# Branch B of the first half, first group: its transposes back and what follows them are released 16 units of the emission clock later

## The chip, the cores and the metric

The kernel runs on one core of one Trainium2 chip. The time is the device time of one execution, in microseconds (us). The program is fixed when it is built: each engine (TensorE, here PE; VectorE, DVE; ScalarE, ACT; GpSimd, POOL; and SyncE's queue SP, which issues the transfers) works through its own list of instructions in order, and engines wait for each other by semaphores.

## The reference, cut to what matters

One layer over 2048 positions with a model width of 1024. An input projection feeds three mixers, their outputs are gated, concatenated, projected back and normalised with the residual. The change touches branch B, whose width is 256:

```
def _conv_module(val, glu_gate, w_dw, b_dw, ln_g, ln_b):
    h = val * jax.nn.sigmoid(glu_gate)
    h = lax.conv_general_dilated(h, w_dw[:, None, :], window_strides=(1,), padding=[(CONV_WIDTH - 1, 0)], ...) + b_dw
    h = _layernorm(h, ln_g, ln_b)
    return jax.nn.silu(h)
...
y_b = _conv_module(b_val, b_glu, conv_w, conv_b, conv_ln_g, conv_ln_b) * jax.nn.silu(b_g)
```

The convolution runs over positions, for each channel by itself, with 31 taps; the layer norm runs over the 256 channels of a position.

## The kernel before, in words

The 2048 positions are worked in two halves (`hf`) of two groups (`gi`) of 512 positions each. In a half, `branch_b` projects for branch B, `sgu` does branch A (both halves, but in the second it comes last), `values` projects the values of branch C (tiles `pm_ci`, eight of them: four for group 0, four for group 1), and `hgrn_unit` does branch C head by head (tiles `pm_f`, `pm_q`, `pm_cg`). Every projection of a 512-wide tile is 8 steps of three matmuls, since each float32 operand is split into a high and a low part (`whi`, `wlo`, `xhi`, `xlo`; on lines 147 and 148 ACT casts the high part of a newly loaded weight and DVE subtracts to get the low one).

The convolution is done by DVE with channels on the partitions: 31 instructions for each pair of group and channel block `ct`, most of them those of line 285 on the tile `acc`. The layer norm needs channels along the free dimension, so `branch_b_norm` has four parts for a group. `part(0)` and `part(1)`, for two of the four 128-position blocks each, transpose `acc` on PE into a PSUM bank `bt`, take mean and variance on DVE (`bst`, `bmv`), the power -0.5 on POOL (`brs`), and write the normalised `bhn` on DVE (line 324). `back(0)` and `back(1)`, for one channel block each, transpose `bhn` back on PE into the bank `bb` (line 330, four transposes of 128x128, which read all four blocks, so the results of both parts), apply SiLU with scale and bias on ACT (`bsy`, line 333), multiply by the gate on DVE (line 334) and store to DRAM through SP (line 232).

Where these parts stand among the other work of an engine is set while the program is written out, by a clock of the builder that has no tie to the time on the chip:

```
def later(dt, fn):
    heapq.heappush(queue, (clock[0] + dt, order[0], fn))
...
def tick(dt):
    clock[0] += dt
    while queue and queue[0][0] <= clock[0]:
        heapq.heappop(queue)[2]()
```

Each step of three 512-wide matmuls is followed by `tick(0.64)`, and whatever has come due is written out at that point. When the last tap of a group has been written out, `conv_taps` puts the four parts into the queue, due after 8, 16, 24 and 32 units (`DNORM` is 8), and a note that the group is done, at 32. The transposes are pinned: PE executes them at the place in its list where they were written out.

Of the kernel before, what the change touches and what calls it, by code (L numbers as in the profile page):

```python
# [42 lines left out]
WB = 5  # L43
NWARM = 9
FIRST = ("00", "x0", "x1", "10", "x2", "01", "x3", "x4", "11", "x5", "x6", "x7")
DTAP, DNORM, DWO = (1.5, 1.35), 8.0, 2.5
DST0, DST, DKT, DPST, DPO, DPT = 4.5, 5.5, 2.5, 2.0, 2.5, 6.0


# [35 lines left out]
def _body(tc, nc, d, ctx):  # L85
# [16 lines left out]
    def bank(tag, bufs, name, shape=(P, 512)):  # L102
        t = ps.tile([P, 512], F32, tag=tag, bufs=bufs, name=name)
        return t
# [15 lines left out]
    def vcol(o):  # L120
        return vec[:, o : o + 1]
# [60 lines left out]
    def later(dt, fn):  # L182
        heapq.heappush(queue, (clock[0] + dt, order[0], fn))
        order[0] += 1
# [11 lines left out]
    def pinned(m):  # L196
        tc.keep_in_program_order(m)
        return m
# [26 lines left out]
    def rstd_of(pl, mv_var, n, tag, scale=1.0, bufs=3):  # L225
        r = pl.tile([P, n], F32, tag=tag, bufs=bufs, name=tag)
        nc.gpsimd.tensor_scalar(r, mv_var, scale, EPS, ALU.mult, ALU.add)  # L227
        nc.gpsimd.tensor_tensor(r, r, nhalf[:, :n], ALU.pow)  # L228
        return r

    def y_store(et, g, t):
        nc.sync.dma_start(y_dr[et, :, g * G : (g + 1) * G], t)
# [37 lines left out]
    def conv_taps(hf, pl, hs, sbg):  # L270
        def normed():
            conv_done[hf] = conv_done.get(hf, 0) + 2

        for gi in range(GPH):
            acc = {}
            for ct in range(2):
                while (ct, gi) not in hs:
                    yield False
                h = hs[ct, gi]
                a = pl.tile([P, G], F32, tag="acc", bufs=4, name=f"acc{hf}_{gi}_{ct}")  # L280
                cw = V_CW + ct * CW
                nc.vector.tensor_scalar(a, h[:, 0:G], vcol(cw), vcol(V_CB + ct), ALU.mult, ALU.add)
                yield True
                for k in range(1, CW):
                    nc.vector.scalar_tensor_tensor(a, h[:, k : k + G], vcol(cw + k), a,  # L285
                                                   ALU.mult, ALU.add)
                    yield True
                acc[ct, gi] = a
            parts = branch_b_norm(hf, pl, sbg, acc, gi)
            for k, part in enumerate(parts):  # L290
                later(DNORM * (k + 1), part)
            later(DNORM * len(parts), normed)

    def conv_start(hf, pl, hs, sbg):
        it = conv_taps(hf, pl, hs, sbg)
        due = [clock[0]]

        def step():
            r = next(it, None)
            if r is not None:  # L300
                due[0] = due[0] + DTAP[hf] if r else clock[0] + DTAP[hf]
                later(due[0] - clock[0], step)

        later(0, step)

    def branch_b_norm(hf, pl, sbg, acc, gi):
        g = hf * GPH + gi
        hn = pl.tile([P, 4, 256], F32, tag="bhn", bufs=1, name=f"bhn{g}")

        def part(cp):  # L310
            mv = pl.tile([P, 2, 2], F32, tag="bmv", bufs=2, name=f"bmv{g}_{cp}")
            pt = bank(("o", "st")[cp], 1, f"bt{g}_{cp}").rearrange("p (c f) -> p c f", f=256)
            for cc in range(2):
                c = cp * 2 + cc
                for ct in range(2):
                    pinned(nc.tensor.transpose(pt[:, cc, ct * P : (ct + 1) * P],
                                               acc[ct, gi][:, c * P : (c + 1) * P], ident))
            for cc in range(2):
                bst = pl.tile([P, 6], F32, tag="bst", bufs=4, name=f"bst{g}_{cp}_{cc}")
                nc.vector.bn_stats(bst, pt[:, cc, :])  # L320
                nc.vector.bn_aggr(mv[:, cc, :], bst)
            rs = rstd_of(pl, mv[:, :, 1], 2, "brs")
            for cc in range(2):
                nc.vector.tensor_scalar(hn[:, cp * 2 + cc, :], pt[:, cc, :], mv[:, cc, 0:1],
                                        rs[:, cc : cc + 1], ALU.subtract, ALU.mult)

        def back(ct):
            pb = bank("tr", 1, f"bb{g}_{ct}")
            for c in range(4):
                pinned(nc.tensor.transpose(pb[:, c * P : (c + 1) * P],  # L330
                                           hn[:, c, ct * P : (ct + 1) * P], ident))
            sy = pl.tile([P, G], F32, tag="bsig", bufs=2, name=f"bsy{g}_{ct}")
            nc.scalar.activation(sy, pb, AF.Silu, bias=vcol(V_CLB + ct), scale=vcol(V_CLG + ct))
            nc.vector.tensor_mul(sy, sy, sbg[ct, gi])
            y_store(2 + ct, g, sy)

        return [lambda: part(0), lambda: part(1), lambda: back(0), lambda: back(1)]
# [713 lines left out]
```

## Time and profile before

| | |
|---|---|
| runs, us | 927.38, 927.51, 928.24 (median 927.51) |
| profiled execution, us | 927.59 |
| its span, first to last instruction, us | 925.8 |
| PE busy | 904.1 us, 98% |
| DVE busy | 713.8 us, 77% |
| ACT busy | 392.2 us, 42% |
| POOL busy | 81.2 us, 9% |
| mean granted clock of TensorE | 0.994 of full speed |

The profiled execution takes 1.79 us more than its span: that much lies before the first and behind the last instruction. Matmuls are pipelined, and their ends are modelled: the duration of a matmul in the rows is longer than the distance to the next one, so work on PE is best counted from start to start. A time in brackets at the end of a row is how long the engine stood idle before it, and whom it waited for. A group of transposes that PE works through in one go is one row with its count.

### The profile page before, as it was taken

The page shows a single profiled execution, that of the slowest core. Times are in us where ns is not written, and L with a number is a line of the kernel's source. Part 1 is how long each engine was busy: PE and PEld are TensorE (multiplying, and loading weights), DVE is VectorE, ACT ScalarE, POOL GpSimd, SP SyncE. Part 2 cuts the span into 40 slices and gives each one's busy share as a digit, 9 for nine tenths or more (in the row PEclk, how much of TensorE's full clock was granted, in tenths as well). Part 3 has the DMA queues.
Part 4 walks back from the last instruction along what each step waited for, and adds up shares of the span by engine and source line. Part 5 has one row for each costly group of instructions (what it writes and reads, how often), then busy time and mean ns, then how long its engine had stood idle before and what let it go on. Part 6 is the DMA issues. An engine that isn't in the chain of part 4 may idle for free.

```text
span 925.8 us, 15037 instructions
## 1 busy us (share of the span) xinstructions
PE 904.1 (98%) x5673; PEld 738.2 (80%) x5673; DVE 713.8 (77%) x1614; ACT 392.2 (42%) x774; POOL 81.2 (9%) x127
## 2 busy tenths in 40 slices
PE   9999998899999999999999999999999999999996
PEld 6889886787777887888888887887889888888885
DVE  5998899935688768997999777778786135898777
ACT  6624355143435336644314334444553343543450
POOL 0001200100010000001000000001012000221122
PEclk9999999899999999999999999999999999999999
DMA  7506786120102103421202011111151498455322
GB/s 259 185 25 224 257 297 248 55 91 24 46 35 69 47 13 110 147 91 64 66 3 92 24 68 36 57 36 58 36 182 58 156 347 292 160 182 183 135 92 91
DMA packets 60808, 107.43 MB, mean 116 GB/s; under 512 B 5312, under 2 KB 21952, under 8 KB 60608
## 3 DMA queue, kind: packets, MB, share of 16 engines
q1 hardware_dynamic: 60736, 106.48, 33.7%
q8 instruction: 44, 0.72, 0.3%
q14 instruction: 28, 0.23, 0.1%
HBM read 75.00 MB, written 31.46 MB: 115 GB/s over the span
## 4 chain that ended last, share of the span: by engine, by line
PE 74%; DVE 13%; DMA 4%; issue 3%; ACT 3%; POOL 2%; SPq 0%; POOLq 0%; DVEq 0%; ACTq 0%
DVE acc L285 5%; PE pm_q L201 3%; PE poz L201 3%; PE poz L203 3%; PE poz L202 3%; PE pm_q L203 3%; PE pm_q L202 3%; PE pm_f L201 3%; PE pm_ci L201 3%; PE pm_ci L203 3%; PE pm_ci L202 3%; PE pm_cg L201 3%; PE pm_f L203 3%; PE pm_f L202 3%; PE pm_cg L202 2%
## 5 line engine op out<-in xcount | busy, mean ns | idle before, releaser
L285 DVE SCALAR_TENSOR_TENSOR acc<-bh,vec,acc 128x512 f32<-128x512 f32 x240 | 172.3, 753 | 2.6
L148 DVE TENSOR_TENSOR wl<-rw,wh 128x512 fp32r<-128x512 f32 x84 | 57.0, 690 | 27.3 <-ACT wh L147 27.1
L147 ACT CAST wh<-rw 128x512 fp32r<-128x512 f32 x84 | 49.9, 618 | 40.7 <-PE pm_f L202 11.1
L201 PE MATMUL pm_f<-xhix,wh 128*128 128x512 f32 x96 | 41.1, 429 | 0.0
L201 PE MATMUL pm_q<-xhix,wh 128*128 128x512 f32 x96 | 40.6, 423 | 0.0
L560 ACT ACTIVATE jk<-po 128x128 f32<-128x128 f32 x64 | 17.7, 277 | 51.9 <-PE po L555 50.9
L201 PE MATMUL pm_cg<-xhix,wh 128*128 128x512 f32 x96 | 39.0, 406 | 0.0
L203 PE MATMUL pm_f<-xhix,wl 128*128 128x512 f32 x96 | 37.7, 393 | 0.0
L202 PE MATMUL pm_q<-xlox,wh 128*128 128x512 f32 x96 | 37.7, 392 | 0.0
L203 PE MATMUL pm_q<-xhix,wl 128*128 128x512 f32 x96 | 37.7, 392 | 0.0
L202 PE MATMUL pm_f<-xlox,wh 128*128 128x512 f32 x96 | 37.6, 392 | 0.0
L203 PE MATMUL pm_cg<-xhix,wl 128*128 128x512 f32 x96 | 37.5, 391 | 0.0
L202 PE MATMUL pm_cg<-xlox,wh 128*128 128x512 f32 x96 | 37.5, 391 | 0.0
L201 PE MATMUL pm_ci<-wh_ci,xhix 128*128 128x512 f32 x96 | 37.4, 389 | 0.0
L203 PE MATMUL pm_ci<-wh_ci,xlox 128*128 128x512 f32 x96 | 37.4, 389 | 0.0
L202 PE MATMUL pm_ci<-wl_ci,xhix 128*128 128x512 f32 x96 | 37.4, 389 | 0.0
L227 POOL TENSOR_SCALAR crs<-ss 128x4 f32<-128x4 f32 x16 | 3.3, 205 | 367.6 <-ACT jk L560 367.6
L355 ACT COPY vh<-pm_ci 128x512 f32<-128x512 f32 x16 | 9.4, 588 | 58.9 <-PE pm_ci L203 58.9
L446 DVE COPY_PREDICATED ST<-msk,sc 64x192 f32<-64x192 int32 (+2 forms) x96 | 28.8, 300 | 5.4 <-PE sc L440 3.1
L503 ACT COPY ST<-sc 64x128 f32<-64x128 f32 x32 | 8.3, 260 | 50.9 <-PE sc L500 50.7
L565 ACT ACTIVATE os<-po,crs 128x128 f32<-128x128 f32 x64 | 18.3, 368 | 24.6 <-POOL crs L228 24.6
L201 PE MATMUL pm_av<-wh_av,xhix 128*128 128x256 f32 x96 | 28.2, 293 | 0.0
(355 smaller groups left out, 2753.1 us busy)
## 6 DMA issues: line engine op xcount, KB each, us to landing
rw<-wf SPq DMA_DIRECT2D x84, 256.0 KB, 3.2
wob<-wo_dr SPq DMA_DIRECT2D x14, 1024.0 KB, 11.5
xr<-x SPq DMA_DIRECT2D x16, 512.0 KB, 3.8
ry<-y_dr SPq DMA_DIRECT2D x32, 256.0 KB, 2.8
out<-xr SPq DMA_DIRECT2D x15, 512.0 KB, 2.6
wo_dr<-wsh SPq DMA_DIRECT2D x28, 256.0 KB, 3.2
wo_dr<-wsl SPq DMA_DIRECT2D x28, 256.0 KB, 2.9
rx<-xT SPq DMA_DIRECT2D x24, 256.0 KB, 3.4
```

The lines of the kernel that those rows point to most:

```text
L147: nc.scalar.copy(hi, src)
L148: nc.vector.tensor_sub(lo, src, hi.bitcast(F32))
L201: nc.tensor.matmul(out, wh, xh, start=first, stop=False, **kw)
L202: nc.tensor.matmul(out, wh, xl, start=False, stop=False, **kw)
L203: nc.tensor.matmul(out, wl, xh, start=False, stop=last, **kw)
L227: nc.gpsimd.tensor_scalar(r, mv_var, scale, EPS, ALU.mult, ALU.add)
L285: nc.vector.scalar_tensor_tensor(a, h[:, k : k + G], vcol(cw + k), a, ALU.mult, ALU.add)
L355: nc.scalar.copy(vh[:, gi * 4 + tt, :], pt)
L446: nc.vector.copy_predicated(ST[rr, :, 64 * m + j0 * b : 64 * m + (j0 + nj) * b], msk[rr, mo : mo + mw].unsqueeze(1).to_broadcast([64, 4, mw]),
L503: nc.scalar.copy(ST[0:64, e:4:2, 64:128], pcv[64 * e : 64 * e + 64])
L560: nc.scalar.activation(jk, po[:, c * P : (c + 1) * P], AF.Square, accum_out=ss[:, c : c + 1])
L565: nc.scalar.mul(os_[:, c * P : (c + 1) * P], po[:, c * P : (c + 1) * P], rs[:, c : c + 1])
```

## The change

The two parts that transpose back, and the note that the group is done, are put into the queue with 16 units more, in the first half's first group alone. The two parts ahead of them keep their due times (8 and 16), and the other three groups keep all of theirs.

```
-DTAP, DNORM, DWO = (1.5, 1.35), 8.0, 2.5
+DTAP, DNORM, DBACK, DWO = (1.5, 1.35), 8.0, 16.0, 2.5
...
             parts = branch_b_norm(hf, pl, sbg, acc, gi)
+            gap = DBACK if hf == 0 and gi == 0 else 0.0
             for k, part in enumerate(parts):
-                later(DNORM * (k + 1), part)
-            later(DNORM * len(parts), normed)
+                later(DNORM * (k + 1) + (gap if k > 1 else 0.0), part)
+            later(DNORM * len(parts) + gap, normed)
```

The due times of this group become 8, 16, 40 and 48. Sixteen units are 25 steps of 0.64, so 75 matmuls. One line more in the file moves later line numbers by one. The lists of POOL and SP hold the same instructions in the same order as before; PE, ACT and DVE differ only in where the two `back` parts stand.

**PE, before, at the first transposes back.** The names say: `pm_ci_0_1` is the second tile of the values (group 0), `pm_ci_0_2` the third; the last number of a name only tells buffers apart.

```order
L201 MATMUL pm_ci_0_1_1572<-wh_ci_3_1504,xhi_first 128x512
L202 MATMUL pm_ci_0_1_1572<-wl_ci_3_1505,xhi_first 128x512
L203 MATMUL pm_ci_0_1_1572<-wh_ci_3_1504,xlo_first 128x512
L330 MATMUL bb_0_1615<-ident,bhn_1308 128x128 x4
L201 MATMUL pm_ci_0_2_1625<-wh_ci_0_1474,xhi_first 128x512
L202 MATMUL pm_ci_0_2_1625<-wl_ci_0_1475,xhi_first 128x512
L203 MATMUL pm_ci_0_2_1625<-wh_ci_0_1474,xlo_first 128x512
```

**PE, now, at the first transposes back.** `pm_ci_1_1` is the sixth tile of the values (group 1).

```order
L201 MATMUL pm_ci_1_1_1732<-wh_ci_0_1474,xhix_266 128x512
L202 MATMUL pm_ci_1_1_1732<-wl_ci_0_1475,xhix_266 128x512
L203 MATMUL pm_ci_1_1_1732<-wh_ci_0_1474,xlox_267 128x512
L331 MATMUL bb_0_1736<-ident,bhn_1308 128x128 x4
L201 MATMUL pm_ci_1_1_1732<-wh_ci_0_1474,xhix_266 128x512
L202 MATMUL pm_ci_1_1_1732<-wl_ci_0_1475,xhix_266 128x512
L203 MATMUL pm_ci_1_1_1732<-wh_ci_0_1474,xlox_267 128x512
```

So `bb_0` stands behind 24 + 24 + 24 + 3 = 75 more matmuls of the values (all of `pm_ci_0_2`, `pm_ci_0_3` and `pm_ci_1_0`, one step of `pm_ci_1_1`). `bb_1` moves by as many, from behind the fifth step of `pm_ci_0_3` to behind the sixth step of `pm_ci_1_2`. With each group of four transposes move its SiLU on ACT, its product on DVE and its store.

**DVE, before, from the last taps of the second group to the weights of branch C.** `acc_1_1` is the second channel block of the half's second group, `bsy` the result of a `back` part, `wl_0` low parts of weights for branch C.

```order
L285 SCALAR_TENSOR_TENSOR acc_1_1_1790<-bh_1_577,vec,acc_1_1_1790 128x512 x4
L334 TENSOR_TENSOR bsy_0_1620<-bsy_0_1620,sbg_0_264 128x512
L285 SCALAR_TENSOR_TENSOR acc_1_1_1790<-bh_1_577,vec,acc_1_1_1790 128x512 x11
L334 TENSOR_TENSOR bsy_1_1697<-bsy_1_1697,sbg_0_516 128x512
L285 SCALAR_TENSOR_TENSOR acc_1_1_1790<-bh_1_577,vec,acc_1_1_1790 128x512 x9
L148 TENSOR_TENSOR wl_0_1860<-rw_0_0_1861,wh_0_1859 128x512
L148 TENSOR_TENSOR wl_0_1860<-rw_0_1_1865,wh_0_1859 128x512
```

**DVE, now, the same stretch.**

```order
L285 SCALAR_TENSOR_TENSOR acc_1_1_1781<-bh_1_577,vec,acc_1_1_1781 128x512 x24
L335 TENSOR_TENSOR bsy_0_1741<-bsy_0_1741,sbg_0_264 128x512
L335 TENSOR_TENSOR bsy_1_1798<-bsy_1_1798,sbg_0_516 128x512
L148 TENSOR_TENSOR wl_0_1860<-rw_0_0_1861,wh_0_1859 128x512
L148 TENSOR_TENSOR wl_0_1860<-rw_0_1_1865,wh_0_1859 128x512
```

The two products move behind all 24 remaining taps, and stand directly ahead of the low parts of the weights for branch C.

## Rows read from the trace of the kernel before

**Rows 1.** The page: span; busy time, share and instructions of each engine.

```profile
span 925.8 us, 15037 instructions
...
PE 904.1 (98%) x5673; PEld 738.2 (80%) x5673; DVE 713.8 (77%) x1614; ACT 392.2 (42%) x774; POOL 81.2 (9%) x127
```

**Rows 2.** Waits of PE, whole span: total us, times, longest us.

```profile
PE bb L330 <- DVE bhn L324: 3.5, 1, 3.5
PE pk L515 <- DVE K L505: 2.2, 2, 1.4
...
PE bt L316 <- ACT os L565: 1.2, 1, 1.2
...
PE pst L531 <- DVE bhn L324: 0.9, 1, 0.9
```

**Rows 3.** Timeline of PE from 160 us: start, us, engine, line, what, count.

```profile
160.65 0.38 PE L330 MATMUL bb<-ident,bhn 128*128 128x128 f32 x2
164.53 0.93 PE L330 MATMUL bb<-ident,bhn 128*128 128x128 f32 x2 [3.50 <-DVE bhn L324]
165.11 0.78 PE L201 MATMUL pm_ci<-wh_ci,xhi_first 128*128 128x512 f32 x1
...
170.36 0.39 PE L201 MATMUL pm_ci<-wh_ci,xhi_first 128*128 128x512 f32 x1
...
176.53 0.60 PE L330 MATMUL bb<-ident,bhn 128*128 128x128 f32 x4
176.88 0.49 PE L201 MATMUL pm_ci<-wh_ci,xhi_first 128*128 128x512 f32 x1
...
200.82 0.39 PE L201 MATMUL pm_f<-xhi_first,wh 128*128 128x512 f32 x1
...
206.26 0.39 PE L201 MATMUL pm_q<-xhi_first,wh 128*128 128x512 f32 x1
```

**Rows 4.** Stretches: us, busy us (instructions) per engine, granted clock, DMA share, GB/s.

```profile
152.00:161.00 9.00, 7.23 (x31) 5.27 (x29) 8.13 (x15) 5.17 (x9) 0.84 (x2) 1.00 0.46 170
161.00:163.50 2.50, 0.03 (x1) 0.00 (x0) 2.06 (x7) 0.43 (x1) 0.84 (x2) 1.00 0.28 105
163.50:164.50 1.00, 0.00 (x0) 0.00 (x0) 0.57 (x2) 0.00 (x0) 1.00 (x3) 0.51 0.25 61
164.50:170.30 5.80, 5.78 (x14) 4.42 (x15) 5.73 (x9) 0.78 (x1) 0.47 (x2) 0.50 0.22 80
170.30:176.50 6.20, 6.20 (x28) 5.02 (x27) 5.95 (x10) 0.59 (x1) 0.00 (x0) 1.00 0.12 45
```

**Rows 5.** Timeline of DVE, from the second part's statistics to branch C's weights.

```profile
160.91 0.76 DVE L320 BATCH_NORM_STATS2 bst<-bt 128x6 f32<-128x256 f32 x2
...
163.93 0.99 DVE L324 TENSOR_SCALAR bhn<-bt,bmv,brs 128x256 f32<-128x256 f32 x2 [0.87 <-POOL brs L228]
...
171.11 0.68 DVE L334 TENSOR_TENSOR bsy<-bsy,sbg 128x512 f32<-128x512 f32 x1
171.72 8.62 DVE L285 SCALAR_TENSOR_TENSOR acc<-bh,vec,acc 128x512 f32<-128x512 f32 x11
...
180.85 7.05 DVE L285 SCALAR_TENSOR_TENSOR acc<-bh,vec,acc 128x512 f32<-128x512 f32 x9
197.60 4.02 DVE L148 TENSOR_TENSOR wl<-rw,wh 128x512 fp32r<-128x512 f32 x6 [9.69 <-ACT wh L147]
```

**Rows 6.** Timeline of ACT: a copy, a SiLU, the weights.

```profile
156.47 0.59 ACT L355 COPY vh<-pm_ci 128x512 f32<-128x512 f32 x1
...
177.16 0.78 ACT L333 ACTIVATE bsy<-bb,vec 128x512 f32<-128x512 f32 x1 [3.25 <-PE bb L330]
...
196.94 1.14 ACT L147 CAST wh<-rw 128x512 fp32r<-128x512 f32 x2 [0.77 <-PE pm_ci L203]
```

**Rows 7.** Timeline of SP's queue: the branch's stores, then loads of weights.

```profile
171.83 9.47 SPq L232 DMA_DIRECT2D y_dr<-bsy  x2
198.32 26.85 SPq L153 DMA_DIRECT2D rw<-wf  x9
```

## Prediction

> **What bounds the kernel now.** I read the page first: PE is busy for 904.1 of 925.8 us, every other engine for far less [rows 1]. A kernel like this gets faster only where PE stands still, does more than it must, or runs at a lower clock. So the next view is the list of PE's waits. It is short, and its longest entry is the line of this change: the transposes back on line 330 wait 3.5 us for `bhn`, once [rows 2]. The timeline of PE shows where: the first two transposes of `bb_0` start at 160.65, the other two only at 164.53, behind 3.50 us of idle time [rows 3]. They read the blocks that `part(1)` normalises. The timeline of DVE shows why these are late: the statistics of that part begin at 160.91, when PE is already at the transposes, and `bhn` is written from 163.93, after a short wait for POOL [rows 5]. DVE works through a backlog in order, and the clock of the builder knows nothing of it.
>
> The view by stretches shows a second cost. The granted clock is 1.00 up to 163.5, although PE has been idle since 161; it is 0.51 to 164.5, 0.50 from there to 170.3, and 1.00 again after that [rows 4]. That is the lower of the two levels, 1.2 GHz instead of 2.4. It fell 2.5 us into the wait, and PE had been matmul upon matmul again for 5.8 us when it rose. So the wait is paid twice, once as idle time, once as slow matmuls behind it.
>
> **The change part by part.** All of it is counted on PE, from start to start.
>
> *What goes.* From the start of `bb_0` to the start of `bb_1` are 176.53 - 160.65 = 15.88 us [rows 3]. In between stand four transposes and 39 matmuls (24 of `pm_ci_0_2`, 15 of `pm_ci_0_3`). The undisturbed pace is that of the 105 matmuls from 176.88 to 200.82 (9 to end `pm_ci_0_3`, 96 of group 1): 23.94 / 105 = 0.228 us each [rows 3]. After the change the 39 follow on directly, and take 39 x 0.228 = 8.89 us. PE is 15.88 - 8.89 = 6.99 us ahead where `bb_1` stood.
>
> *What is paid again.* The four transposes of `bb_0` come later. Undisturbed, four of them cost 176.88 - 176.53 = 0.35 us, the price of `bb_1` [rows 3]. `bb_1` itself costs the same at either place. The sum is 6.99 - 0.35 = 6.64 us.
>
> *The same by cause.* The wait, 3.50. Twelve slow matmuls from 165.11 to 170.36, 5.25 us instead of 12 x 0.228 = 2.74, so 2.51. The first transposes, 0.38 for two and 165.11 - 164.53 = 0.58 for two instead of 0.35 for all, so 0.61. That is 6.62; the 0.02 left over is a pace slightly above 0.228 from 170.36 to 176.53 [rows 3].
>
> *Whether the new places wait.* `bb_0` now comes up at 160.65 + 75 x 0.228 = 177.75. The last `bhn` is there at 163.93 + 0.99 = 164.92 [rows 5], nearly 13 us before. `bb_1` comes up at 177.75 + 0.35 + 39 x 0.228 = 186.99; the one bank of `bb` must have been emptied by then. A SiLU began 0.63 us after the transposes and took 0.78 [rows 3, 6], so `bb_0` is read by 179.2.
>
> *Whether another wait lay hidden behind the old one.* `pm_ci_0_2` uses weights that `pm_ci_0_1` has used already. The projections rotate through three banks; `pm_ci_0_3`, which now starts at 160.65 + 24 x 0.228 = 166.1, takes the bank of `pm_ci_0_0`, copied out from 156.47 in 0.59 [rows 6]. I find none.
>
> *What is queued behind the moved steps.* On DVE the two products (0.61 each, from 171.11 to 171.72 [rows 5]) move behind the taps. DVE has no pause until 180.85 + 7.05 = 187.90; without the products the taps end at about 186.7. The first product runs to 187.3. The second waits for its SiLU, which ends at 186.99 + 0.63 + 0.78 = 188.40, and is done at 189.1. Behind it in the list are the low parts of branch C's weights. They started at 197.60, after 9.69 us of idle time, held by ACT, which was held by PE [rows 5, 6]. Shifted by 6.64 they start at 190.96, so 1.9 us remain. If this cover were gone, the six parts (4.02 us) would still end at 195.0, and `pm_q`, which needs the first of them, moves from 206.26 to 199.62 [rows 3]: another 4.6 us. I cost this at nothing. On SP the second store of `bsy`, issued at about 189.2, stands ahead of nine loads that began at 198.32 [rows 7], so at 191.68 now; nothing too. On ACT the second SiLU stands ahead of the copy of `pm_ci_1_2`, which is complete later than `bb_1` anyway.
>
> *What the rest makes of it.* PE's other waits in the branch C stages total 2.2, 1.2 and 0.9 us [rows 2], and they are for work that PE's own earlier results set off, so they travel with it. From 190.96 on DVE again follows ACT, and ACT follows PE; everything behind should stand as before, 6.64 us earlier.
>
> The profiled execution took 927.59, so it would take 920.95. The median of the runs shown, 927.51, lies 0.08 under that execution: 920.87. I forecast 920.9.
>
> *A rule that speaks against the price of transposes.* Rows put four transposes between dense matmuls at 0.35 us, and the matmuls behind them at the pace of the full clock [rows 3]. The Trainium skill ("TensorE: Matmul & The Clock Gate", Part 4: PE-mode transpose) reports about 275 ns for each transpose in one kernel, and that transposes don't count towards the full clock as other work does. By its figure four would be an estimated 1.1 us, the gain 5.9 and the time 921.6; the trace does not agree for a group in the middle of dense work, and the row is used.
>
> **The rivals.**
>
> *The clock falls anyway.* PE also stood idle for 9.00 - 7.23 = 1.77 us between 152 and 161 [rows 4], ahead of the transposes, and this stays. If that were enough to bring the clock down, a slow stretch of 6.8 us (163.5 to 170.3) would cost half of that, 3.4 us, and the time would be 924.3. Against it: the granted clock was 1.00 all through those gaps and for 2.5 us of the long one [rows 4].
>
> *Part is given back in branch C.* PE arrives 6.6 us earlier and meets DVE or ACT less far ahead. For it: DVE's spare time shrinks from 9.69 to 1.9 us. Against it: PE needs nothing of it for 4.6 us more. Two more waits like the longest of those for `K`, 1.4 us [rows 2], would make it 923.7.
>
> *The wait only moves.* The transposes, or the matmuls now in their place, wait for something that the stall has covered. Then there is no change, 927.5. For it speaks only that waits behind a stall can't be seen; `bhn` is 13 us early, and the banks are free.
>
> *Slower.* The second product stands at the head of DVE's list, ahead of branch C's low parts, and DVE waits there for ACT. It costs nothing until its SiLU is 1.9 + 4.6 = 6.5 us later than worked out; from then on PE waits for the weights at `pm_q`, a us for a us. It is slower than before from 6.5 + 6.64 = 13.1 us on; at 16 us it would be 927.5 + 2.9 = 930.4. Ahead of that SiLU on ACT stand only copies of 0.59 us [rows 6], so I see nothing that could delay it so far.
>
> **How the numbers follow.** Chances: the forecast 0.83, the clock 0.05, given back in part 0.04, the wait only moves 0.04, slower 0.04. The measurement can tell about 0.2%, 1.9 us, from no change. Faster by more than that: 0.83 + 0.05 + 0.04 = 0.92; the same 0.04; slower 0.04. For the range, below: one of the remaining small waits, 0.9 us [rows 2], may vanish as engines shift against each other, and the fastest run shown lies 0.1 under the median: 919.9. Above: one further wait of 1.4 us, and the slowest run, 928.24, lies 0.7 over the median: 923.0. This leaves out nearly all of the other four cases, 0.17 together.
>
> **What would show it.** In the profile of the changed kernel the wait of line 331's transposes for `bhn` of 3.5 us is gone, the twelve matmuls stand 0.228 apart and the granted clock stays at 1.00 from 161 to 188. `bb_0` starts near 177.7, `bb_1` near 187.0, `pm_f` near 194.2. DVE has a wait of about 1 us for the second SiLU and an idle time of about 2 us ahead of the low parts. From there to the end each landmark is 6.6 us earlier. I am wrong if the clock dips somewhere else, if a wait appears at `pm_q` or among the loads behind the store of `bsy`, or if the shift of 6.6 us at `pm_f` shrinks on the way to the end.

## The result and the profile after

The changed kernel ran in 921.56 us (median of 6 runs, 920.55 to 923.13), the kernel before in 927.88 beside it (6 runs, 926.60 to 928.79). The ratio is 0.9937 (95% interval 0.9926 to 0.9948): 5.8 us gained, with 4.8 to 6.9 for the interval, where 6.64 were forecast. The two medians lie 6.3 us apart; gains below are taken from the ratios unless medians are named. The forecast of 920.9 and the median differ by 0.7 us, and the median lies in the range. The profiled execution is the slowest of the six, 923.13 with a span of 921.4; its rows below show a slow stretch of PE.

PE's waits, the longest of them (total us, times, longest). The wait for `bhn` at the transposes, which led the list before [rows 2], is gone:

```profile
PE pk L516 <- DVE K L506: 2.2, 2, 1.4
...
PE bt L317 <- ACT os L566: 1.2, 1, 1.2
PE pm_ci L202 <- DVE wl_ci L148: 1.2, 2, 0.9
...
PE pm_ci L201 <- ACT wh_ci L147: 1.0, 1, 1.0
PE pst L532 <- DVE bhn L325: 0.8, 1, 0.8
```

The stretches of [rows 4], same columns. From 158 us on PE has no pause and the full clock; but between 154 and 158 the granted clock is 0.57, where the kernel before had 1.00 in its profile:

```profile
154.00:158.00 4.00, 3.35 (x8) 2.67 (x9) 4.00 (x7) 3.06 (x5) 0.00 (x0) 0.57 0.78 254
158.00:161.00 3.00, 3.00 (x15) 2.44 (x14) 3.00 (x6) 0.00 (x0) 0.00 (x0) 1.00 0.02 7
161.00:188.00 27.00, 27.00 (x122) 22.35 (x121) 24.90 (x39) 3.72 (x6) 2.32 (x5) 1.00 0.09 30
```

The timeline of PE, with the landmarks of [rows 3]:

```profile
153.20 0.50 PE L201 MATMUL pm_ci<-wh_ci,xhi_first 128*128 128x512 f32 x1 [0.96 <-ACT wh_ci L147]
154.65 0.79 PE L202 MATMUL pm_ci<-wl_ci,xhi_first 128*128 128x512 f32 x1 [0.95 <-DVE wl_ci L148]
155.24 0.63 PE L203 MATMUL pm_ci<-wh_ci,xlo_first 128*128 128x512 f32 x1
...
157.80 0.40 PE L203 MATMUL pm_ci<-wh_ci,xlo_first 128*128 128x512 f32 x1
...
179.14 0.60 PE L331 MATMUL bb<-ident,bhn 128*128 128x128 f32 x4
179.49 0.48 PE L201 MATMUL pm_ci<-wh_ci,xhix 128*128 128x512 f32 x1
...
188.48 0.60 PE L331 MATMUL bb<-ident,bhn 128*128 128x128 f32 x4
...
195.77 0.39 PE L201 MATMUL pm_f<-xhi_first,wh 128*128 128x512 f32 x1
```

Two gaps of about 1 us, ahead of the change and in both kernels, were followed here by matmuls 0.43 us apart, the lower of the two levels. So `bb_0` starts 1.4 us later than worked out (177.75). The later landmarks are 1.5 and 1.6 us late (186.99 and 194.18 were worked out), so between them all goes nearly as forecast: from `bb_0` to `bb_1` 9.34 us, worked out as 9.24. `pm_f` is 200.82 - 195.77 = 5.05 us ahead of the kernel before; from there to the end of the span this execution takes 0.6 us more (921.4 - 195.77 = 725.6 against 725.0).

DVE's timeline, as in [rows 5]:

```profile
163.97 0.99 DVE L325 TENSOR_SCALAR bhn<-bt,bmv,brs 128x256 f32<-128x256 f32 x2 [0.87 <-POOL brs L228]
...
166.14 20.84 DVE L285 SCALAR_TENSOR_TENSOR acc<-bh,vec,acc 128x512 f32<-128x512 f32 x27
186.90 0.69 DVE L335 TENSOR_TENSOR bsy<-bsy,sbg 128x512 f32<-128x512 f32 x1
189.93 0.69 DVE L335 TENSOR_TENSOR bsy<-bsy,sbg 128x512 f32<-128x512 f32 x1 [2.34 <-ACT bsy L334]
192.54 4.01 DVE L148 TENSOR_TENSOR wl<-rw,wh 128x512 fp32r<-128x512 f32 x6 [1.92 <-ACT wh L147]
```

`bhn` is written when it was before (163.97 against 163.93). The products stand behind the taps; the second waits 2.34 us for its SiLU, as late as the transposes are, and 1.92 us stay free ahead of the weights of branch C. The list of PE's waits has none for these weights.

### The profile page after: what moved, and what is told of

Read it like the earlier page. It is cut to its first block, busy times and chain, and to the rows that moved or that the text cites. A ratio compares the mean times of both kernels' runs of the same rounds, so it can differ in the third digit from the quotient of the medians.

```text
span 921.4 us, 15037 instructions
## 1 busy us (share of the span) xinstructions
PE 902.0 (98%) x5673; PEld 735.7 (80%) x5673; DVE 714.3 (78%) x1614; ACT 392.6 (43%) x774; POOL 81.9 (9%) x127
## 4 chain that ended last, share of the span: by engine, by line
PE 74%; DVE 12%; DMA 5%; issue 3%; ACT 2%; POOL 2%; SPq 0%; POOLq 0%; DVEq 0%; ACTq 0%
DVE acc L285 5%; PE pm_q L201 3%; PE pm_ci L202 3%; PE pm_ci L203 3%; PE pm_ci L201 3%; PE pm_q L203 3%; PE pm_q L202 3%; PE pm_f L201 3%; PE poz L201 3%; PE pm_cg L201 3%; PE poz L203 3%; PE poz L202 3%; PE pm_f L203 3%; PE pm_cg L202 3%; PE pm_cg L203 3%
```

## The experiments

Ratios are to the kernel before, run beside each on the same chip, with their 95% intervals. There were three sets: the first four experiments below (median of the kernel before 927.27), the next four (927.60) and the last three (927.89). Every profile is a single execution.

**The change once more.** No edit.

> The changed kernel once more. Theory (the removed wait is worth 6.6 us, and the half-clock stretch from 154.4 to 157.8 us that its first profile shows belongs to that execution alone): median 921 to 922; the granted clock is 1.00 from 152 to 188 us and the first matmul of pm_f starts near 194.2. Rival (the change brings the slow stretch with it): the granted clock from 152 to 161 us is again about 0.8, pm_f starts near 195.8, and the profiled execution takes about 923.

Measured: 923.35 us (920.94 to 925.19), ratio 0.9956 (0.9940 to 0.9972). This median lies above the range that was forecast. The rival was right for the profile: the slow stretch is there again, `pm_f` starts at 196.46, and the profiled execution takes 924.25.

```profile
196.46 0.39 PE L201 MATMUL pm_f<-xhi_first,wh 128*128 128x512 f32 x1
```

```profile
152.00:161.00 9.00, 7.05 (x22) 5.12 (x22) 8.12 (x15) 5.58 (x9) 1.16 (x2) 0.81 0.59 193
161.00:201.00 40.00, 40.00 (x182) 33.10 (x181) 31.30 (x48) 11.41 (x18) 2.32 (x5) 1.00 0.23 77
```

**Four units instead of sixteen.** An edit of the changed kernel:

```
-DTAP, DNORM, DBACK, DWO = (1.5, 1.35), 8.0, 16.0, 2.5
+DTAP, DNORM, DBACK, DWO = (1.5, 1.35), 8.0, 4.0, 2.5
```

> The two back parts are released 4 units later instead of 16: 18 matmuls, 4.1 us. Theory (only the wait for bhn counts, and it ends at 164.5 us): the transposes come up at about 164.7, wait for 0.2 us at most, and the time is that of the change, 921 to 922. Rival (the distance counts, or that DVE's products stand behind all taps): a quarter of the gain, about 926; here nine taps stand ahead of the first product, twelve between the two, and three behind.

Measured: 922.98 us (919.83 to 926.74), ratio 0.9955 (0.9939 to 0.9971), the same as sixteen units beside it. PE's timeline has `bb_0` in one piece, with no wait:

```profile
164.96 0.40 PE L203 MATMUL pm_ci<-wh_ci,xlo_first 128*128 128x512 f32 x1
165.20 0.60 PE L331 MATMUL bb<-ident,bhn 128*128 128x128 f32 x4
```

So neither the distance nor the place of the products on DVE is what helps, but that `bhn` (written from 164.39 in this execution) is there.

**Two steps, 1.28 units.** The same line with 1.28.

> The two back parts are released two steps later: 6 matmuls, 1.37 us, so that some 2.1 us of the wait stay. Theory with the clock as a cost of its own: the wait now ends before the 2.5 us after which the clock fell in the kernel before; no slow stretch follows, and the gain is 1.4 plus about 2.9, so 923.5. If the clock falls all the same, or the slow matmuls were no cost of this wait: 1.4 alone, 926.4. Rival (the distance counts): 2 of 25 steps, 927.3.

Measured: 924.88 us (923.00 to 927.27), ratio 0.9974 (0.9964 to 0.9983), so 2.4 us: more than the 1.4 us of the six matmuls, less than 4.3. The profile, the slowest of the twelve executions, can't tell how the clock behaves in a short wait, because in that execution it had fallen before:

```profile
155.59 0.80 PE L201 MATMUL pm_ci<-wh_ci,xhi_first 128*128 128x512 f32 x1 [0.95 <-ACT wh_ci L147]
157.03 0.80 PE L202 MATMUL pm_ci<-wl_ci,xhi_first 128*128 128x512 f32 x1 [0.65 <-DVE wl_ci L148]
...
166.88 0.85 PE L331 MATMUL bb<-ident,bhn 128*128 128x128 f32 x4
```

```profile
154.00:158.00 4.00, 2.40 (x5) 1.31 (x6) 3.13 (x6) 3.96 (x7) 1.16 (x2) 0.68 0.90 267
```

The weights came 2.4 us later here than in the kernel before (157.03 against 154.61), for PE and DVE alike: `bhn` was written from 166.35, not 163.93. Slow matmuls from 157 to 162 brought PE another 2.4 us late to the transposes, and so the wait was used up. A slow stretch ahead of the transposes and the wait at them are not two costs to be added: the one shortens the other.

**`part(1)` earlier, the back parts where they were.** An edit of the kernel before:

```
             for k, part in enumerate(parts):
-                later(DNORM * (k + 1), part)
+                due = DNORM * (k + 1)
+                if k == 1 and hf == 0 and gi == 0:
+                    due = 12.0
+                later(due, part)
```

> The kernel before, with the back parts where they were and part(1) of this group due after 12 units instead of 16, which moves its statistics and its bhn ten places up in DVE's list. Theory (the wait is the cause, not the place of the transposes): bhn is written about 5 us earlier, before PE comes to the transposes at 160.6, the wait is gone, and the time is that of the change, 921 to 922. Rival (the later place of the transposes, or of the products behind the taps, is what helps): no gain, 927.5.

Measured: 922.77 us (921.93 to 924.04), ratio 0.9953 (0.9941 to 0.9966), the gain of the change beside it. The second pair of `bhn` comes 5 us earlier on DVE, and PE does not wait at the transposes:

```profile
155.81 0.75 DVE L323 BATCH_NORM_STATS2 bst<-bt 128x6 f32<-128x256 f32 x2
...
158.88 0.99 DVE L327 TENSOR_SCALAR bhn<-bt,bmv,brs 128x256 f32<-128x256 f32 x2 [0.87 <-POOL brs L228]
```

```profile
153.91 0.50 PE L201 MATMUL pm_ci<-wh_ci,xhi_first 128*128 128x512 f32 x1 [0.96 <-ACT wh_ci L147]
155.35 0.50 PE L202 MATMUL pm_ci<-wl_ci,xhi_first 128*128 128x512 f32 x1 [0.94 <-DVE wl_ci L148]
...
161.39 0.60 PE L333 MATMUL bb<-ident,bhn 128*128 128x128 f32 x4
```

**`part(1)` later.** The same edit with 20.0 in place of 12.0, to make the wait longer.

> The opposite of the earlier run on part(1): the kernel before with part(1) of this group due after 20 units instead of 16, the back parts where they were. Its statistics and its bhn stand about four taps further down in DVE's list. Theory: bhn comes about 2.7 us later, the wait at bb_0 grows from 3.5 to about 6.2 us, and the time goes up by as much, to 930. Rival (the wait is hidden somewhere behind): no change, 927.3.

Measured: 931.65 us (929.59 to 933.10), ratio 1.0038 (1.0024 to 1.0053), so 3.5 us slower, with 2.2 to 4.9. The wait is 6.9 us, 3.4 more than before and more than the 6.2 expected:

```profile
168.60 0.93 PE L333 MATMUL bb<-ident,bhn 128*128 128x128 f32 x2 [6.92 <-DVE bhn L327]
...
180.00 0.60 PE L333 MATMUL bb<-ident,bhn 128*128 128x128 f32 x4
```

The longer wait passes into the time, us for us as far as the interval tells.

**Work for PE in the wait.** To hold the clock up without removing the wait, matmuls of zeros in the kernel before, into a bank `pf` that nothing reads:

```
+NFILL = 34
...
+    fill = cst.tile([P, 192], BF16, name="fill")
+    nc.vector.memset(fill, 0.0)
...
+            pf = bank("sc", 2, f"fill{g}") if g == 0 and ct == 0 else None
             for c in range(4):
+                if c == 2 and pf is not None:
+                    for _ in range(NFILL):
+                        pinned(nc.tensor.matmul(pf[:, :192], fill[:, :P], fill, start=True, stop=True))
                 pinned(nc.tensor.transpose(pb[:, c * P : (c + 1) * P],
...
```

> The kernel before with 34 matmuls of zeros (128x192, about 0.1 us each, 3.4 us in all) put between the first two and the last two transposes of bb_0, so that PE has work in most of the wait for bhn; the wait itself stays. Theory (the clock is a cost of its own, about 2.9 us): the granted clock stays at 1.00 after 161 us, and the time falls by 2.5 to 3 us, to 924 to 925, though bhn is as late as before. Rival (the slow stretch belongs to what comes after, or costs nothing): no gain, 927.3, or slower by what the matmuls run over the wait.

Measured: 926.02 us (923.31 to 927.79), ratio 0.9979 (0.9969 to 0.9989), so 1.9 us with 1.0 to 2.9. PE's timeline:

```profile
162.20 0.38 PE L337 MATMUL bb<-ident,bhn 128*128 128x128 f32 x2
162.41 2.97 PE L336 MATMUL fill<-fill 128*128 128x192 bf16 x34
165.22 0.38 PE L337 MATMUL bb<-ident,bhn 128*128 128x128 f32 x2
```

```profile
154.00:158.00 4.00, 3.42 (x9) 2.75 (x10) 4.00 (x7) 2.98 (x5) 0.00 (x0) 0.64 0.75 249
...
163.50:164.50 1.00, 1.00 (x15) 1.00 (x14) 0.61 (x2) 0.00 (x0) 1.00 (x3) 1.00 0.20 61
164.50:170.30 5.80, 5.80 (x35) 4.97 (x33) 5.73 (x9) 0.78 (x1) 0.43 (x2) 1.00 0.25 83
```

The clock stays at 1.00 through the wait and behind it. The clock had a price of its own, but the test is not clean: in this execution too it had fallen at 154 (0.64 from 154 to 158), so PE came 1.55 us late to the transposes. `bhn` was written from 163.89, as ever; the other pair began 0.60 us after that in the kernel before [rows 3, 5], so the matmuls of zeros ran some 0.7 us too long.

**Three buffers ahead of the change.** The gaps of PE at 150 to 155 us are waits for the values' weights, whose casts on ACT stand behind a cast of the output weights, which waits for a store to free its buffer. The kernel before, ACT's timeline:

```profile
149.56 0.62 ACT L147 CAST wsh<-wr 128x512 fp32r<-128x512 f32 x1 [3.03 <-DMA wo_dr<-wsh]
150.08 0.62 ACT L147 CAST wh_ci<-rwci 128x512 fp32r<-128x512 f32 x1
```

The edit:

```
-                hi = pl.tile([P, 512], F32R, tag="wh", bufs=2, name=f"wsh{j}_{blk}")
-                lo = pl.tile([P, 512], F32R, tag="wl", bufs=2, name=f"wsl{j}_{blk}")
+                hi = pl.tile([P, 512], F32R, tag="wh", bufs=3, name=f"wsh{j}_{blk}")
+                lo = pl.tile([P, 512], F32R, tag="wl", bufs=3, name=f"wsl{j}_{blk}")
```

> The changed kernel with three buffers instead of two each for the high and low parts of the output weights (lines with wsh and wsl), whose casts on ACT wait for stores and stand ahead of the casts of the values' weights. Theory (the gaps of 1 to 3 us that PE has at 150 to 158 us come from there, and bring the clock down there in some executions): these gaps shrink, the granted clock is 1.00 from 150 to 161, and the time is 1 to 3 us under that of the change, 919 to 921. Rival (the gaps come from the transfers' own rate): no gain, 922 to 923.

> The kernel before with the same three buffers, and without the later release. Theory (the wait for bhn ends when DVE's list gets to it, not when PE comes): where PE comes earlier it only waits longer, so there is little gain over the kernel before, 926 to 927.5. Rival (DVE follows PE there): the same gain as in the changed kernel, 1 to 3 us.

Measured side by side: with the change 919.01 us (917.36 to 919.74), ratio 0.9903 (0.9888 to 0.9917); without it 925.37 (923.58 to 925.68), ratio 0.9968 (0.9955 to 0.9980). In the first PE has no gap and the full clock throughout:

```profile
150.00:158.00 8.00, 8.00 (x36) 6.59 (x36) 7.57 (x13) 2.37 (x4) 0.39 (x1) 1.00 0.49 151
158.00:201.00 43.00, 43.00 (x195) 35.54 (x195) 32.32 (x50) 13.30 (x20) 2.39 (x5) 1.00 0.25 80
```

Here the change is worth 925.37 - 919.01 = 6.4 us by the medians and (0.9968 - 0.9903) x 927.6 = 6.0 us by the ratios, with 3.5 to 8.5 from the ends of their intervals. My expectation for the second kernel was wrong: it gains 3.0 us. PE comes to the transposes at 157.90 instead of 160.65, and waits about as long as before, because the statistics on DVE also move, to 158.22 from 160.91:

```profile
157.90 0.38 PE L330 MATMUL bb<-ident,bhn 128*128 128x128 f32 x2
161.88 0.86 PE L330 MATMUL bb<-ident,bhn 128*128 128x128 f32 x2 [3.60 <-DVE bhn L324]
...
172.97 0.60 PE L330 MATMUL bb<-ident,bhn 128*128 128x128 f32 x4
```

```profile
158.22 0.75 DVE L320 BATCH_NORM_STATS2 bst<-bt 128x6 f32<-128x256 f32 x2
```

**Three buffers and the matmuls of zeros, without the change.** Both edits above.

> The kernel before with three buffers for the output weights' parts and the 34 matmuls of zeros in the wait for bhn, which stays. Without the gaps at 150 to 158 us the clock's share should show by itself. Theory: the granted clock is 1.00 from 150 to 201 us, and the time is 1.5 to 3 us under that of three buffers alone (ratio 0.9968 to the kernel before), so a ratio of 0.994 to 0.995. Rival (the clock costs nothing here): 0.9968 again.

Measured: 923.08 us (921.69 to 923.44), ratio 0.9946 (0.9933 to 0.9958). Against 0.9968 with the buffers alone, from another set, this is 0.0022 x 927.6 = 2.0 us for the clock; the two intervals just touch. What is left for the wait and what hangs on it is 0.9946 - 0.9903, so 4.0 us, and 3.0 us against the 0.9914 of the next experiment, which is from the same set. The clock is 1.00, while the wait is filled up to its last 0.78 us:

```profile
158.20 2.97 PE L336 MATMUL fill<-fill 128*128 128x192 bf16 x34
161.96 0.78 PE L337 MATMUL bb<-ident,bhn 128*128 128x128 f32 x2 [0.78 <-DVE bhn L327]
...
171.43 0.60 PE L337 MATMUL bb<-ident,bhn 128*128 128x128 f32 x4
```

```profile
161.00:163.50 2.50, 1.59 (x10) 1.06 (x7) 2.14 (x4) 0.72 (x1) 1.40 (x4) 1.00 0.00 0
163.50:164.50 1.00, 1.00 (x6) 0.84 (x5) 1.00 (x3) 0.06 (x1) 0.00 (x0) 1.00 0.07 16
```

**Three buffers and four units; three buffers for the high parts alone.**

> The release 4 units later instead of 16, with three buffers. Theory (only the wait counts, and DVE's list moves with PE's): the same as 16 units with three buffers, a ratio of 0.990 to the kernel before, some 919 us. Rival (where PE no longer has gaps ahead, 4 units are too few and part of the wait comes back): 0.992 to 0.994.

> The changed kernel with three buffers for the high parts alone. Theory (it is ACT's wait for the stores of the high parts that holds the values' weights): the same gain as with three of each, a ratio of 0.990. Rival (DVE's low parts hold them as well): between 0.9905 and 0.995.

Measured: 919.33 us (918.35 to 922.65), ratio 0.9914 (0.9897 to 0.9930), and 919.43 (918.22 to 920.77), ratio 0.9910 (0.9896 to 0.9923). Neither can be told from the 0.9903 of three buffers each with sixteen units. With the high parts alone PE still waited 2.03 us for a low part of the values' weights in the profile, so that single execution does not show ACT's share freed of DVE's.

```profile
154.55 0.50 PE L202 MATMUL pm_ci<-wl_ci,xhi_first 128*128 128x512 f32 x1 [2.03 <-DVE wl_ci L148]
```

## Why the prediction was right, and where its sum was off

**The wait.** Right, and shown from four sides: it is gone when the transposes come later by 16 or by 4 units, or when `bhn` comes earlier, all three with the same gain in one set (4.1 to 4.4 us), and 3.4 us more of it made the kernel 3.5 us slower. That the new places would not wait, that no other wait lay behind the old one, and that DVE's queue would leave 1.9 us in front of branch C's weights (1.92 measured), came out as worked out.

**The clock.** Right in kind: with work for PE in the wait the clock stays up, and the time falls although the wait is still there. The size, 2.51 us, came from one profile, and it differs from execution to execution. From the second pair of `bb_0` to the start of `bb_1` the kernel before took 176.53 - 164.53 = 12.00 us [rows 3], with `part(1)` late it was 11.40, with three buffers and no later release 11.09, and 9.47 with the zeros as well, where the clock stayed up. So the slow stretch cost 2.5, 1.9 and 1.6 us in these three. The times with the zeros give 1.9 and 2.0 us.

**What the sum left out.** The rival "the clock falls anyway" got 0.05. It is what happened in both profiles of the changed kernel, ahead of the transposes, and cost 1.4 us in the first, not the 3.4 of the rival. The argument against it, that the clock had been at 1.00 through those gaps in the kernel before, rested on one execution. Without extra buffers, the clock is down between 154 and 158 us in four of eight profiles: the change twice, 1.28 units, and the zeros in the wait; not in the kernel before, 4 units, `part(1)` early, `part(1)` late. I also took the two costs as independent. In the kernel before, a slow stretch at 154 only eats into the wait at 160, since `bhn` comes when DVE gets to it (163.9 in the kernel before, the changed one and the one with zeros); in the changed kernel it is paid in full. That the kernel before hides such a stretch is read from those rows and from the run with 1.28 units; no run forced one, and the mean granted clock on record for each execution does not say where in the span it fell.

**How near the number is.** That 921.56 lies so near 920.9 is in part luck: the same kernel gave 923.35 beside another set, above the range. The gains are 5.8 us in the first set, 4.1 in the second, and 6.0 with three buffers, where the gaps are gone. The second is what the wait and the transposes alone make in the sum (3.50 + 0.61), so there nothing of the clock's 2.51 is seen. A slow stretch ahead of the transposes in a part of the executions would explain that, and that the kernel without gaps comes nearest to 6.64; but the intervals of the three overlap, so their order is not shown. The other price that the prediction weighed for the transposes gives 921.6, which is the median; that is chance, for in the changed kernel four of them go through in 179.49 - 179.14 = 0.35 us again.

**The other rivals.** Nothing shows a gain given back further down: from the first matmul of `pm_f` to the end of the span the profiles of all kernels here take 724.7 to 726.3 us, 725.0 before and 726.0 with `part(1)` late, neither of which has the change, 725.6 and 726.0 in the two of the changed kernel. No wait appeared at `pm_q`, and the second product held up nobody.

**The better version.** Three buffers and the later release run in 919.0 us, a ratio of 0.9903 to the kernel before, with 0.9903 / 0.9937 = 0.997 to the change alone (from different sets).

## What to carry to other kernels

Where an engine's list is fixed when the program is built, a wait of one in-order engine for another's backlog can be removed by putting the waiting step later or the awaited one earlier; both paid the same here, and a quarter of the distance gave the same gain. Count such a gain from start to start on the engine that sets the end, and ask of each term whether something ahead in the list could use up the same slack: a delay that the old wait hid is paid in full once the wait is gone. Size a cost of the clock from several profiles, not from one: here one and the same stretch of work cost between 1.6 and 2.5 us.

## What the runs showed of the hardware

The granted clock does not follow the length of a gap alone. It fell after gaps of 0.96 and 0.95 us in the first profile of the change, stayed at 1.00 after gaps of 0.96 and 0.94 us when `part(1)` came early, and stayed there after a gap of 2.03 us with three high buffers. The 34 matmuls of zeros, 192 columns of bf16 each with a weight load of its own, took 165.22 - 162.41 = 2.81 us, 0.083 us each, and in both profiles that have them the granted clock was 1.00 in the wait and behind it.
